# FFN input GEMMs by one level of Strassen for all 1024 tokens, the residual kept in DRAM tiles

## The chip, the cores and the metric

One NeuronCore of a Trainium2 chip runs the whole program. The metric is the device time of one execution in microseconds; a lower time is better.

## The reference

One encoder layer on x of 1024 tokens by 1024 features, all in float32. FFN1, a mixer, FFN2 and a last RMSNorm follow each other:

```python
def swiglu(x, w_in, w_out):
    gate, up = jnp.split(x @ w_in, 2, axis=-1)
    return (jax.nn.silu(gate) * up) @ w_out
...
x = x + 0.5 * swiglu(rmsnorm(x, ffn1_norm_g[l]), ffn1_w_in[l], ffn1_w_out[l])
...
x = x + merged @ w_mix_out[l]
x = x + 0.5 * swiglu(rmsnorm(x, ffn2_norm_g[l]), ffn2_w_in[l], ffn2_w_out[l])
...
return rmsnorm(x, final_norm_g)
```

`w_in` is 1024 by 5632 (gate columns, then up columns), `w_out` 2816 by 1024. The mixer (an mLSTM branch and a gating branch) lies between the two FFNs and is not touched.

## The kernel before, in words

Activations stand with features on the 128 partitions and 512 tokens along a row, so the sequence is done in two halves of 512 tokens. Each float32 operand is split into a high and a low float32r part (`split`, and `load_unit` for weights: one ScalarE cast and one VectorE subtraction), and a product is three matmuls (`PROD`: high by high, high by low, low by high). One matmul has a 128x128 piece of weights as the loaded operand and 128x512 activations as the streamed one.

`ffn` (L256) runs once for each half and each FFN, four times in all. It goes through 22 tiles of 128 hidden features in three blocks of 8, 8 and 6 (`BLOCKS`). `ffn_in` (L239) takes two tiles at once: 8 feature tiles of x by 3 matmuls, for two gate and two up banks of PSUM, then Silu on ScalarE (L244), the product on VectorE (L250) and a `split`. After a block the output projection accumulates in PSUM over the block's tiles (L271), and VectorE adds it to the residual `xs`, which stays in SBUF (L275). The last block of the last half goes in two parts of 256 tokens (`parts=2`), so that the end is short.

Work that isn't needed at once goes into the list `todo` and is taken from it by `spread`, one piece between two blocks of matmuls: the transposes of x, the normalisation of the next half (`normed`, `later=True`). RMS statistics are gathered by `Stats` (squares on ScalarE, sums on VectorE); `rstd` and `bcast` then make a chain of two small TensorE steps with small VectorE and ScalarE steps between (L198 to L221). All DMA is issued by SyncE (SP). A scheduler orders each engine's instructions by priority and by free buffers; each engine then runs its own list in that order and waits at an instruction whose operands or buffers are not ready.

Of the kernel before, what the change touches and what calls it, by code (L numbers as in the profile page):

```python
# [19 lines left out]
BLOCKS = [(0, 8), (8, 8), (16, 6)]  # L20
# [9 lines left out]
def block_body(ctx, tc, x, ffn1_norm_g, ffn1_w_in, ffn1_w_out, mix_norm_g, w_mix_in, mlstm_conv_w,  # L30
# [9 lines left out]
    wp = ctx.enter_context(tc.tile_pool(name="wp", bufs=3))  # L40
    bigp = ctx.enter_context(tc.tile_pool(name="bigp", bufs=16))
    tp = ctx.enter_context(tc.tile_pool(name="tp", bufs=5))
# [12 lines left out]
    open_psum(f1, 1, mm=3, po=3, ml=2)  # L55

    def t512():
        return tp.tile([P, NH], F32, tag="t512", name="t512")

    def psm():  # L60
        return bank("ml")

    def load_tokens(h):
        ts = []
        for t in range(4):
            xt = bigp.tile([P, D], F32, tag="big", name="xtok")
            nc.sync.dma_start(out=xt, in_=x[h * NH + t * P:h * NH + (t + 1) * P, :])
            ts.append(xt)
        return ts
# [31 lines left out]
    xd = [[tc.dram_tile([P, KT, NH], F32, name=f"xd{s}{h}") for h in range(2)] for s in range(2)]  # L101

    def load_unit(w_rows, ks, c0, extra=None):
# [9 lines left out]
        w = wp.tile([P, 2, n, nc_], F32R, tag="w", name="w")  # L113
# [4 lines left out]

    PROD = ((0, 0), (0, 1), (1, 0))
# [65 lines left out]
    class Stats:  # L185
# [25 lines left out]
        def bcast(self):  # L211
# [7 lines left out]
            bc = sp.tile([P, NH], F32, tag="bc", name="bc", bufs=1)  # L219
# [19 lines left out]
    def ffn_in(w_in, f0, xn, hp, ready=None):  # L239
        gb = feature_pair(w_in, f0 * P, xn, "mm", ready=ready)  # L240
        sg = []
        for j in range(2):
            t = t512()
            A.activation(out=t, in_=gb[j], func=AF.Silu)  # L244
            sg.append(t)
        ub = feature_pair(w_in, DFF + f0 * P, xn, "mm")
        hs = []
        for j in range(2):
            hf = t512()
            V.tensor_tensor(out=hf, in0=sg[j], in1=ub[j], op=ALU.mult)  # L250
            h = hp.tile([P, 2, NH], F32R, tag="h", name="h")
            split(hf, h)
            hs.append(h)
        return hs

    def ffn(w_in, w_out, xn, xs, hp, final, hooks={}, ready=None, parts=1):  # L256
        for bi, (f0, n) in enumerate(BLOCKS):
            hs = []
            for f in range(f0, f0 + n, 2):
                hs += ffn_in(w_in, f, xn, hp, ready if f == 0 else None)  # L260
                spread()
                spread()
            if bi in hooks:
                hooks[bi]()
            last = bi == len(BLOCKS) - 1
            np_ = parts if last else 1
            kg = tuple(tuple(range(a, min(a + 4, n))) for a in range(0, n, 4))
            for part in range(np_):
                ts = slice(part * NH // np_, (part + 1) * NH // np_)
                for d in range(0, KT, 2):  # L270
                    ob = feature_pair(w_out[f0 * P:(f0 + n) * P, :], d * P, hs, "po", kg, ts=ts)  # L271
                    spread()
                    for j in range(2):
                        xt = xs[d + j][:, ts]
                        V.scalar_tensor_tensor(out=xt, in0=ob[j], scalar=0.5, in1=xt, op0=ALU.mult, op1=ALU.add)  # L275
                        if last:
                            final(d + j, part, xt)
# [3 lines left out]

    wsT = cst.tile([P, 4, P], F32, name="wsT")
    t1 = cst.tile([P, KT, P], F32, name="t1")
    future = cst.tile([P, P], F32, name="future")
    bif = cst.tile([P, 8], F32, name="bif")
    nc.sync.dma_start(out=bif[:, 0:4], in_=mlstm_b_igate[0].partition_broadcast(P))
    nc.sync.dma_start(out=bif[:, 4:8], in_=mlstm_b_fgate[0].partition_broadcast(P))

    def setup():
        wraw = t512()  # L290
        nc.sync.dma_start(out=wraw.rearrange("p (g s) -> p g s", g=4), in_=sgu_w_s[0].rearrange("g t s -> t g s"))
        ps = psm()
        for g in range(4):
            PE.transpose(out=ps[:, g * P:(g + 1) * P], in_=wraw[:, g * P:(g + 1) * P], identity=ident)
        V.tensor_copy(out=wsT.rearrange("p g t -> p (g t)"), in_=ps)
        G.memset(wsT[64:P, :, 0:64], 0.0)
        bsb = t512()
        nc.sync.dma_start(out=bsb, in_=sgu_b_s[0].rearrange("g t -> (g t)").partition_broadcast(P))
        ps = psm()
        PE.matmul(out=ps, lhsT=ones, rhs=wsT.rearrange("p g t -> p (g t)"), start=True, stop=True)  # L300
        for ct in range(KT):
            g = ct // 2
            V.scalar_tensor_tensor(out=t1[:, ct, :], in0=ps[:, g * P:(g + 1) * P], scalar=pc("sb", ct),
                                   in1=bsb[:, g * P:(g + 1) * P], op0=ALU.mult, op1=ALU.add)
        G.memset(future, 0.0)
        G.affine_select(out=future, in_=future, compare_op=ALU.is_ge, fill=1e30, base=0, pattern=[[1, P]],
                        channel_multiplier=-1)

    def mix(mx, xnm):
# [305 lines left out]
        for half in range(2):  # L615
            xn = xnm[half]
            if half == 0:
                gz, gt = sgu_v(xn)
# [184 lines left out]
```

## Time and profile before

| | |
|---|---|
| runs | 2406.90, 2407.29, 2408.02 us, median 2407.29 |
| profiled execution, span | 2406.5 us |
| TensorE (PE) busy | 2383.2 us, 99% |
| weight loads (PEld) busy | 2012.1 us, 84% |
| VectorE (DVE) busy | 1174.0 us, 49% |
| ScalarE (ACT) busy | 890.1 us, 37% |
| GpSimd (POOL) busy | 3.9 us |
| DMA | 253.69 MB, 105 GB/s |

The span is the time from the first to the last instruction of the one execution that the profiler recorded; the median of the runs is 0.8 us above it. Busy time counts every instruction but register, branch, semaphore and DMA-issuing ones. Weight loads run under the matmuls.

### The profile page before, as it was taken

The numbers are of one execution on the slowest core, as the hardware profiler recorded it, in microseconds if no ns is written. First come the engines' busy times: TensorE is split into PE (matmuls) and PEld (weight loads), VectorE is DVE, ScalarE is ACT, GpSimd is POOL, SyncE is SP. The second block draws the span as 40 slices with busy tenths as digits, with TensorE's granted clock in tenths as the row PEclk, the third lists the DMA queues.
The fourth block names the chain that finished last, engine by engine and source line by source line (L and its number), as shares of the span: only waits on it lengthen the run. The fifth ranks groups of instructions, "written<-read, shape, count | busy, mean of one in ns | idle before, by whom it ended". The sixth has DMA issues, their size and how long they took to land. (4 is left out here: it accounts for less than half of the span.)

```text
span 2406.5 us, 28857 instructions
## 1 busy us (share of the span) xinstructions
PE 2383.2 (99%) x11817; PEld 2012.1 (84%) x11817; DVE 1174.0 (49%) x1864; ACT 890.1 (37%) x1178; POOL 3.9 (0%) x15
## 2 busy tenths in 40 slices
PE   8999999999999999999999999999999999999998
PEld 7888888888888988888889888888888888888887
DVE  4444434344335657556646666564344335333336
ACT  4223223323224445444434554453323223222224
POOL 0000000000000000000000000000000000000000
PEclk9999999999999999999999999999999999999999
DMA  5322324333324324332352342327333334333333
GB/s 176 92 92 91 98 87 136 105 97 97 96 88 141 97 79 123 97 87 81 95 160 80 96 123 80 101 75 227 97 96 97 97 92 127 106 97 98 97 93 123
DMA packets 240547, 253.69 MB, mean 105 GB/s; under 512 B 11160, under 2 KB 227864, under 8 KB 240416
## 3 DMA queue, kind: packets, MB, share of 16 engines
q1 hardware_dynamic: 240416, 251.86, 34.7%
q8 instruction: 92, 1.51, 0.3%
q14 instruction: 39, 0.32, 0.0%
HBM read 239.21 MB, written 12.62 MB: 105 GB/s over the span
## 5 line engine op out<-in xcount | busy, mean ns | idle before, releaser
L138 PE MATMUL mm<-xn,w 128*128 128x512 f32 x6528 | 1510.7, 390 | 0.5 <-DVE w L115 0.5
L138 PEld LDWEIGHTS mm<-xn,w 128*128 128x128 f32 x6528 | 1218.5, 188 | 249.5 <-issue 1.4
L115 DVE TENSOR_TENSOR w<-raw,w 128x1024 fp32r<-128x1024 f32 (+2 forms) x426 | 508.5, 1194 | 844.6 <-ACT w L114 844.3
L114 ACT CAST w<-raw 128x1024 fp32r<-128x1024 f32 (+2 forms) x426 | 436.9, 1026 | 882.4 <-PE mm L138 320.3
L138 PE MATMUL po<-h,w 128*128 128x512 f32 (+1 forms) x2256 | 493.0, 378 | 0.0
L138 PEld LDWEIGHTS po<-h,w 128*128 128x128 f32 x2256 | 403.6, 188 | 80.7 <-issue 0.5
L152 PE MATMUL mm<-w,xn 128*128 128x256 f32 x1344 | 164.8, 283 | 0.3
L152 PEld LDWEIGHTS mm<-w,xn 128*128 128x128 f32 x1344 | 162.9, 192 | 1.4 <-DVE w L115 0.7
L244 ACT ACTIVATE t<-mm 128x512 f32<-128x512 f32 x88 | 52.6, 598 | 152.5 <-PE mm L138 152.5
L275 DVE SCALAR_TENSOR_TENSOR x<-po,x 128x512 f32<-128x512 f32 (+1 forms) x104 | 66.8, 649 | 82.8 <-PE po L138 82.7
L171 ACT CAST h<-t 128x512 fp32r<-128x512 f32 x88 | 54.3, 618 | 106.2 <-DVE t L250 106.2
L138 PE MATMUL po<-mh,w 128*128 128x512 f32 x384 | 87.5, 389 | 0.0
L250 DVE TENSOR_TENSOR t<-t,mm 128x512 f32<-128x512 f32 x88 | 60.5, 687 | 50.0 <-PE mm L138 50.0
L138 PEld LDWEIGHTS po<-mh,w 128*128 128x128 f32 x384 | 71.9, 188 | 14.9
L172 DVE TENSOR_TENSOR h<-t,h 128x512 fp32r<-128x512 f32 x88 | 60.5, 687 | 30.4 <-ACT h L171 30.3
L453 DVE SCALAR_TENSOR_TENSOR t<-pre,par,t 128x512 f32<-128x512 f32 x96 | 72.0, 750 | 2.2
L575 ACT ACTIVATE t<-mm 128x512 f32<-128x512 f32 x48 | 28.7, 598 | 48.0 <-PE mm L138 47.9
L448 ACT COPY pre<-mm 128x512 f32<-128x512 f32 x32 | 18.8, 587 | 61.1 <-PE mm L138 61.1
L577 DVE TENSOR_TENSOR M<-M,t 128x512 f32<-128x512 f32 x32 | 22.1, 690 | 33.2 <-ACT t L575 33.2
L196 DVE TENSOR_TENSOR acc<-acc,t 128x512 f32<-128x512 f32 (+1 forms) x56 | 34.6, 618 | 4.4 <-ACT t L195 4.3
L575 ACT ACT_TABLE_LOAD x25 | 32.1, 1283 | 0.4
L171 ACT CAST xn<-t 128x512 fp32r<-128x512 f32 x40 | 24.3, 619 | 21.1 <-DVE t L229 20.9
(180 smaller groups left out, 1048.5 us busy)
## 6 DMA issues: line engine op xcount, KB each, us to landing
raw<-in_ffn_w_in_dram SPq DMA_DIRECT2D x176, 512.0 KB, 3.5
raw<-in_w_mix_in_dram SPq DMA_DIRECT2D x124, 512.0 KB, 3.8
raw<-in_ffn_w_out_dram SPq DMA_DIRECT2D x84, 512.0 KB, 3.4
xr<-xd SPq DMA_DIRECT2D x32, 256.0 KB, 3.6
raw<-in_w_mix_out_dram SPq DMA_DIRECT2D x16, 512.0 KB, 4.3
raw<-in_ffn_w_out_dram SPq DMA_DIRECT2D x20, 256.0 KB, 3.1
xtok<-in_x_dram SPq DMA_DIRECT2D x8, 512.0 KB, 5.9
xd<-x SPq DMA_DIRECT2D x16, 256.0 KB, 3.1
```

Of the source, the lines that this page charges most:

```text
L114: A.copy(out=w[:, 0, 0:n, :], in_=raw[:, 0:n, :])
L115: V.tensor_tensor(out=w[:, 1, 0:n, :], in0=raw[:, 0:n, :], in1=w[:, 0, 0:n, :].bitcast(F32), op=ALU.subtract)
L138: PE.matmul(out=banks[j], lhsT=w[:, a, i, j * P:(j + 1) * P], rhs=act[k][:, b, ts], start=(k == first and pi == 0), stop=(k == last and pi ...
L152: PE.matmul(out=o, lhsT=act[k][:, b, t * P:(t + 1) * P], rhs=w[:, a, i, :], start=(t % 2 == 0 and k == 0 and pi == 0), stop=(t % 2 == 1 an ...
L171: A.copy(out=dst[:, 0, :], in_=src)
L172: V.tensor_tensor(out=dst[:, 1, :], in0=src, in1=dst[:, 0, :].bitcast(F32), op=ALU.subtract)
L196: V.tensor_tensor(out=self.acc, in0=self.acc, in1=sq, op=ALU.add)
L244: A.activation(out=t, in_=gb[j], func=AF.Silu)
L250: V.tensor_tensor(out=hf, in0=sg[j], in1=ub[j], op=ALU.mult)
L275: V.scalar_tensor_tensor(out=xt, in0=ob[j], scalar=0.5, in1=xt, op0=ALU.mult, op1=ALU.add)
L453: V.scalar_tensor_tensor(out=t, in0=pre[:, j:j + NH], scalar=pc("cw%d" % j, cc), in1=t, op0=ALU.mult, op1=ALU.add)
L575: A.activation(out=t, in_=b[j], func=fn)
```

## The change

Both halves of the sequence now go through an FFN together, in the new class `Ffn`. For a tile f of 128 hidden features the input GEMM is a 2x2 block product: the rows are gate and up, the inner blocks are the two halves of the 1024 features, the columns are the two halves of the tokens. Strassen's scheme in Winograd's form takes seven block products of 12 matmuls in place of eight. `operands` builds sums and differences of the activation blocks (`t1` to `t4`) once per FFN; `group` builds those of the weight blocks (`s1` to `s4`) for each tile and adds the products up on VectorE. For the first five tiles `first_product` computes two of the seven products ahead, while the operands are being built. The hidden tiles go in blocks of 3 (and 2), and `down` adds a block's output projection to a residual that lies in DRAM tiles: for each of 16 tiles of 128x512, GpSimd issues a load (L366) into a buffer of the pool `cp` and a store (L369) out of it. The last block (`last`) keeps the tiles in SBUF. The bits of the diff that carry this:

```diff
-BLOCKS = [(0, 8), (8, 8), (16, 6)]
+NF = DFF // P
+BLOCKS = [(0, 3), (3, 3), (6, 3), (9, 3), (12, 3), (15, 3), (18, 2), (20, 2)]
+AHEAD = 5
...
+        xv = x[h * NH:(h + 1) * NH, :].rearrange("(t p) d -> p t d", p=P)
+        for i in range(4):
+            xt = bigp.tile([P, 4, 2, P], F32, tag="big", name="xtok")
+            for j in range(2):
+                nc.sync.dma_start(out=xt[:, :, j, :], in_=xv[:, :, (4 * j + i) * P:(4 * j + i + 1) * P])
...
-    xd = [[tc.dram_tile([P, KT, NH], F32, name=f"xd{s}{h}") for h in range(2)] for s in range(2)]
+    xd = [[[tc.dram_tile([P, NH], F32, name=f"xd{s}{h}{d}") for d in range(KT)] for h in range(2)] for s in range(3)]
...
+            self.tx, self.hp, self.wp, self.sp_ = pool("tx", 12), pool("hp", 8), pool("fw", 4), pool("fs", 3)
+            self.cp = pool("cp", 6)
...
+        def raw(self, f, d, both):
+            r = rawp.tile([P, 4, 2, P], F32, tag="raw", name="raw")
+            rs = slice(d * NH, (d + 1) * NH)
+            for j in range(2 if both else 1):
+                nc.sync.dma_start(out=r[:, :, j, :], in_=self.w_in[rs, j * DFF + f * P:j * DFF + (f + 1) * P]
+                                  .rearrange("(k p) c -> p k c", p=P))
+            return r
+
+        def unit(self, src, n=4):
+            w = self.wp.tile([P, 2, n, P], F32R, tag="fw", name="fw")
+            A.copy(out=w[:, 0], in_=src)
+            V.tensor_tensor(out=w[:, 1], in0=src, in1=w[:, 0].bitcast(F32), op=ALU.subtract)
+            return w
+
+        def prod(self, bank, w, b, start, stop):
+            for i in range(4):
+                for pi, (x, y) in enumerate(PROD):
+                    PE.matmul(out=bank, lhsT=w[:, x, i, :], rhs=self.B[b][i][:, y, :],
+                              start=(start and i == 0 and pi == 0), stop=(stop and i == 3 and pi == 2),
+                              skip_group_check=True)
+
+        def combine(self, a, b, op):
+            s = self.sp_.tile([P, 4, P], F32, tag="s", name="s")
+            V.tensor_tensor(out=s, in0=a, in1=b, op=op)
+            return s
+
+        def first_product(self, f):
+            e = self.hp.tile([P, 2, NH], F32, tag="h", name="early")
+            r1, r2 = self.raw(f, 0, False), self.raw(f, 1, False)
+            w1, w2 = self.unit(r1[:, :, 0, :]), self.unit(r2[:, :, 0, :])
+            a = bank("mm")
+            self.prod(a, w1, "11", True, False)
+            A.copy(out=e[:, 0, :], in_=a)
+            self.prod(a, w2, "21", False, True)
+            A.activation(out=e[:, 1, :], in_=a, func=AF.Silu)
+            self.early[f] = e
+
+        def group(self, f):
+            r1, r2 = self.raw(f, 0, True), self.raw(f, 1, True)
+            a11, a21 = evens(r1)
+            a12, a22 = evens(r2)
+            e = self.early.pop(f, None)
+            if e is None:
+                w = self.unit(a11)
+                a = bank("mm")
+                self.prod(a, w, "11", True, False)
+                p1 = self.c512()
+                A.copy(out=p1, in_=a)
+            else:
+                p1 = e[:, 0, :]
+            s1 = self.combine(a21, a22, ALU.add)
+            s2 = self.combine(s1, a11, ALU.subtract)
+            w = self.unit(s2)
+            b = bank("mm")
+            self.prod(b, w, "t2", True, True)
+            u2 = self.c512()
+            V.tensor_tensor(out=u2, in0=b, in1=p1, op=ALU.add)
+            if e is None:
+                w = self.unit(a12)
+                self.prod(a, w, "21", False, True)
+                sg1 = self.c512()
+                A.activation(out=sg1, in_=a, func=AF.Silu)
+            else:
+                sg1 = e[:, 1, :]
+            yield
+            s3 = self.combine(a11, a21, ALU.subtract)
+            w = self.unit(s3)
+            b = bank("mm")
+            self.prod(b, w, "t3", True, True)
+            u3 = self.c512()
+            V.tensor_tensor(out=u3, in0=b, in1=u2, op=ALU.add)
+            w = self.unit(s1)
+            d = bank("mm")
+            self.prod(d, w, "t1", True, False)
+            c22 = self.c512()
+            V.tensor_tensor(out=c22, in0=d, in1=u3, op=ALU.add)
+            w = self.unit(a22)
+            b = bank("mm")
+            self.prod(b, w, "t4", True, True)
+            V.tensor_tensor(out=u3, in0=b, in1=u3, op=ALU.add)
+            h1 = self.hp.tile([P, 2, NH], F32R, tag="h", name="h")
+            V.tensor_tensor(out=u3, in0=u3, in1=sg1, op=ALU.mult)
+            split(u3, h1)
+            s4 = self.combine(a12, s2, ALU.subtract)
+            w = self.unit(s4)
+            self.prod(d, w, "22", False, True)
+            V.tensor_tensor(out=u2, in0=d, in1=u2, op=ALU.add)
+            A.activation(out=u2, in_=u2, func=AF.Silu)
+            h2 = self.hp.tile([P, 2, NH], F32R, tag="h", name="h")
+            V.tensor_tensor(out=c22, in0=c22, in1=u2, op=ALU.mult)
+            split(c22, h2)
+            self.hs.append((h1, h2))
+            yield
+
+        def down(self, f0, n, hs, src, dst):
+            for d in range(0, KT, 2):
+                raw = rawp.tile([P, n, 2 * P], F32, tag="raw", name="raw")
+                nc.sync.dma_start(out=raw, in_=self.w_out[f0 * P:(f0 + n) * P, d * P:(d + 2) * P]
+                                  .rearrange("(k p) c -> p k c", p=P))
+                for j in range(2):
+                    w = self.unit(raw[:, :, j * P:(j + 1) * P], n)
+                    for t in range(2):
+                        xt = self.c512()
+                        G.dma_start(out=xt, in_=src[t][d + j])
+                        o = self.down_mm(w, n, [h[t] for h in hs], slice(0, NH))
+                        V.scalar_tensor_tensor(out=xt, in0=o, scalar=0.5, in1=xt, op0=ALU.mult, op1=ALU.add)
+                        G.dma_start(out=dst[t][d + j], in_=xt)
...
+
+        def down_mm(self, w, n, hs, ts):
+            o = bank("mm")[:, ts]
+            for i in range(n):
+                for pi, (x, y) in enumerate(PROD):
+                    PE.matmul(out=o, lhsT=w[:, x, i, :], rhs=hs[i][:, y, ts], start=(i == 0 and pi == 0),
+                              stop=(i == n - 1 and pi == 2))
+            return o
+
+        def last(self, f0, n, hs, src, final, parts, hook):
...
+            for t in range(2):
+                xl = []
+                for part in range(parts[t]):
+                    ts = slice(part * NH // parts[t], (part + 1) * NH // parts[t])
+                    for d in range(KT):
+                        if part == 0:
+                            if d % 2 == 0:
+                                xl.append(self.tx.tile([P, 2, NH], F32, tag="tx", name="xl"))
+                            G.dma_start(out=xl[-1][:, d % 2, :], in_=src[t][d])
+                        o = self.down_mm(ws[d], n, [h[t] for h in hs], ts)
+                        xt = xl[d // 2][:, d % 2, ts]
+                        V.scalar_tensor_tensor(out=xt, in0=o, scalar=0.5, in1=xt, op0=ALU.mult, op1=ALU.add)
+                        final(t, d, part, xt)
+                        spread()
+                hook(t, [xl[d // 2][:, d % 2, :] for d in range(KT)])
+
+        def run(self, src, final, parts, hook):
+            self.hs = []
+            blocks = list(BLOCKS)
+            pend = None
+            for bi, (f0, n) in enumerate(blocks):
+                for f in range(f0, f0 + n):
+                    g = self.group(f)
+                    next(g)
+                    if pend is not None:
+                        self.down(*pend)
+                        pend = None
+                    next(g)
...
+                hs, self.hs = self.hs, []
+                if bi < len(blocks) - 1:
+                    pend = (f0, n, hs, src if bi == 0 else xd[2], xd[2])
+                else:
+                    self.last(f0, n, hs, xd[2], final, parts, hook)
+
+        def operands(self, i, get):
+
+            b12, b22, b11, b21 = get(0, i, 1), get(1, i, 1), get(0, i, 0), get(1, i, 0)
+
+            def put(key, src):
+                pool, tag = (self.tx, "tx") if key in ("t1", "t2", "t3") else (bigp, "big")
+                t = pool.tile([P, 2, NH], F32R, tag=tag, name="b")
+                split(src, t)
+                self.B.setdefault(key, []).append(t)
+
+            t3 = self.c512()
+            V.tensor_tensor(out=t3, in0=b22, in1=b12, op=ALU.subtract)
+            put("t3", t3)
+            V.tensor_tensor(out=b12, in0=b12, in1=b11, op=ALU.subtract)
+            put("t1", b12)
+            V.tensor_tensor(out=t3, in0=b22, in1=b12, op=ALU.subtract)
+            put("t2", t3)
+            V.tensor_tensor(out=b21, in0=b21, in1=t3, op=ALU.subtract)
+            put("22", b22)
+            put("t4", b21)
...
+        tok[1] = load_tokens(1)
+        ffn1.first_product(0)
+        scales(1)
+        for i in range(4):
+            ffn1.first_product(i + 1)
+            for d in (i, i + 4):
+                residual(0, d)
+                residual(1, d)
+            ffn1.operands(i, get)
...
+        def get2(j, i, t):
+            b = ffn2.c512()
+            d = 4 * j + i
+            G.dma_start(out=b, in_=xd[1][t][d])
+            V.scalar_tensor_tensor(out=b, in0=b, scalar=pc("g2", d), in1=bcs[t], op0=ALU.mult, op1=ALU.mult)
+            return b
+
+        ffn2.first_product(0)
+        for i in range(4):
+            ffn2.first_product(i + 1)
+            ffn2.operands(i, get2)
```

Three places show how the order of instructions moves. In its rows the part ahead of the arrow is written, the part behind it read; a number behind a name tells one buffer from another.

TensorE where FFN1 ends and the mixer begins, of the kernel before: `h` is the hidden tile, `xn` the normalised input of the mixer, `acc` the statistics of the second half.

```order
L138 MATMUL mm<-xn,w 128x512 x384
L138 MATMUL po<-h,w 128x512 x192
L138 MATMUL mm<-xn,w 128x512 x288
L138 MATMUL po<-h,w 128x512 x144
L165 MATMUL mm<-w,xn 128x264 x22
L201 MATMUL ml<-ones,acc 128x1 x4
L165 MATMUL mm<-w,xn 128x264 x30
L218 MATMUL ml<-t_4980,ones 128x512
```

The same place of the changed kernel:

```order
L280 MATMUL mm<-b,fw 128x512 x48
L376 MATMUL mm<-h,wl 128x512 x66
L210 MATMUL ml<-ones,acc 128x1 x4
L376 MATMUL mm<-h,wl 128x512 x25
L227 MATMUL ml<-t_5856,ones 128x512
L376 MATMUL mm<-h,wl 128x512 x5
L174 MATMUL mm<-w,xn 128x264 x8
L210 MATMUL ml<-ones,acc 128x1 x4
L174 MATMUL mm<-w,xn 128x264 x17
```

The statistics of the first half now come inside the last 96 matmuls of FFN1 and not half an FFN earlier, and the first mixer GEMM follows 5 matmuls behind the broadcast of its scale.

TensorE where the mixer ends and FFN2 begins, of the kernel before (`mh` is the mixer's output):

```order
L138 MATMUL po<-mh,w 128x512 x192
L138 MATMUL mm<-xn,w 128x512 x14
L201 MATMUL ml<-ones,acc 128x1 x4
L138 MATMUL mm<-xn,w 128x512 x17
L218 MATMUL ml<-t_12813,ones 128x512
L138 MATMUL mm<-xn,w 128x512 x353
```

The same place of the changed kernel; `fw` are weight units, `b` the operands that `operands` builds:

```order
L147 MATMUL po<-mh,w 128x512 x192
L210 MATMUL ml<-ones,acc 128x1 x4
L227 MATMUL ml<-t_13900,ones 128x512
L280 MATMUL mm<-xn,fw 128x512 x120
L280 MATMUL mm<-b,fw 128x512 x192
L376 MATMUL mm<-h,fw 128x512 x144
```

No FFN matmul stands any more between the mixer's last matmul and the two small steps of the statistics; 120 matmuls stand between these and the first one that needs the built operands.

GpSimd's queue in the second `down` of FFN1 (before, GpSimd issued no DMA); `xd_148` and its like are residual tiles in DRAM, `c` a buffer of `cp`:

```order
L366 DMA c<-xd_148 128x512
L366 DMA c<-xd_156 128x512
L366 DMA c<-xd_149 128x512
L366 DMA c<-xd_157 128x512
L369 DMA xd_148<-c 128x512
L369 DMA xd_156<-c 128x512
L366 DMA c<-xd_150 128x512
L369 DMA xd_149<-c 128x512
L366 DMA c<-xd_158 128x512
L369 DMA xd_157<-c 128x512
```

Four loads go ahead; from there a load stands behind the store of the tile three before its own, and its buffer is free when the store of the tile four before has landed.

## Rows read from the trace of the kernel before

**Rows 1.** Page: engines' busy us (share) xinstructions; clock granted in 40 slices.

```profile
PE 2383.2 (99%) x11817; PEld 2012.1 (84%) x11817; DVE 1174.0 (49%) x1864; ACT 890.1 (37%) x1178; POOL 3.9 (0%) x15
...
PEclk9999999999999999999999999999999999999999
```

**Rows 2.** Longest wait of TensorE in the program: us, times, longest.

```profile
PE po L675 <- DVE dg L671: 8.1, 1, 8.1
```

**Rows 3.** Busy us by engine in three stretches; then clock, DMA share, GB/s.

```profile
0.00:20.00 20.00, 10.89 (x68) 10.22 (x69) 8.77 (x38) 11.57 (x29) 1.31 (x10) 1.00 0.54 187
100.00:700.00 600.00, 599.96 (x2662) 494.19 (x2661) 247.83 (x307) 177.70 (x221) 0.40 (x2) 1.00 0.32 99
2360.00:2406.50 46.50, 37.82 (x312) 36.15 (x310) 32.66 (x81) 20.95 (x40) 0.00 (x0) 0.95 0.44 136
```

**Rows 4.** TensorE's groups by form: busy us, mean ns, idle before.

```profile
L138 PE MATMUL mm<-xn,w 128*128 128x512 f32 x6528 | 1510.7, 390 | 0.5 <-DVE w L115 0.5
...
L138 PE MATMUL po<-h,w 128*128 128x512 f32 x1968 | 455.7, 392 | 0.0
...
L138 PE MATMUL po<-h,w 128*128 128x256 f32 x288 | 37.3, 283 | 0.0
...
L752 PE MATMUL ml<-ident,x 128*128 128x128 f32 x64 | 11.3, 282 | 0.7 <-DVE x L275 0.6
...
L218 PE MATMUL ml<-t,ones 128*128 128x512 f32 x10 | 5.2, 600 | 0.3 <-DVE gT L413 0.3
...
L675 PE MATMUL ml<-dg,xtok 128*128 128x128 f32 x32 | 4.2, 278 | 0.5 <-DVE xn L679 0.5
```

**Rows 5.** VectorE's groups by form: busy us, mean ns, idle before.

```profile
L275 DVE SCALAR_TENSOR_TENSOR x<-po,x 128x512 f32<-128x512 f32 x88 | 60.6, 691 | 80.4 <-PE po L138 80.3
...
L250 DVE TENSOR_TENSOR t<-t,mm 128x512 f32<-128x512 f32 x88 | 60.5, 687 | 50.0 <-PE mm L138 50.0
...
L196 DVE TENSOR_TENSOR acc<-acc,t 128x512 f32<-128x512 f32 x42 | 28.8, 685 | 4.3 <-ACT t L195 4.2
...
L229 DVE SCALAR_TENSOR_TENSOR t<-x,par,bc 128x512 f32<-128x512 f32 x24 | 17.1, 744 | 2.3 <-ACT bc L220 2.3
...
L115 DVE TENSOR_TENSOR w<-raw,w 128x512 fp32r<-128x512 f32 x20 | 13.8, 692 | 46.2 <-ACT w L114 46.2
...
L275 DVE SCALAR_TENSOR_TENSOR x<-po,x 128x256 f32<-128x256 f32 x16 | 6.2, 418 | 2.4 <-PE po L138 2.4
```

**Rows 6.** ScalarE's groups by form: busy us, mean ns, idle before.

```profile
L114 ACT CAST w<-raw 128x512 fp32r<-128x512 f32 x20 | 12.4, 621 | 63.6 <-issue 42.6 <-PE mm L138 15.6 <-PE po L138 5.4
```

**Rows 7.** DMA issues of 256 KB to or from the residual, us to landing.

```profile
xr<-xd SPq DMA_DIRECT2D x32, 256.0 KB, 3.6
...
xd<-x SPq DMA_DIRECT2D x16, 256.0 KB, 3.1
...
xd<-xr SPq DMA_DIRECT2D x16, 256.0 KB, 5.3
x<-xd SPq DMA_DIRECT2D x16, 256.0 KB, 4.7
```

**Rows 8.** Timeline of the start: start us, us, engine, line, [idle].

```profile
11.81 0.29 DVE L671 TENSOR_SCALAR dg<-ident,r 128x128 f32<-128x128 f32 x1
...
19.76 21.61 PE L138 MATMUL mm<-xn,w 128*128 128x512 f32 x94 [0.53 <-DVE w L115]
```

**Rows 9.** Timeline, end of the mixer: last statistics add to broadcast.

```profile
1665.41 0.68 DVE L196 TENSOR_TENSOR acc<-acc,t 128x512 f32<-128x512 f32 x1
...
1668.75 0.88 DVE L215 TENSOR_SCALAR t<-ident,rstd 128x128 f32<-128x128 f32 x4
...
1672.16 0.59 ACT L220 COPY bc<-ml 128x512 f32<-128x512 f32 x1 [1.35 <-PE ml L218]
```

**Rows 10.** Timeline, start of the mixer: VectorE beside a GpSimd memset.

```profile
758.02 2.39 DVE L215 TENSOR_SCALAR t<-ident,rstd 128x128 f32<-128x128 f32 x4
...
758.34 1.93 POOL L323 MEMSET v<- 128x2064 f32 x1 [275.29 <-DMA xd<-x]
```

More of the change, by code (lines that the diff above doesn't have):

```diff
@@ L237, in normed @@
         return res
[L239 to L260, printed above, removed]
-                spread()
[L262 to L271, printed above, removed]
-                    spread()
[L273 to L277, printed above, removed]
+    def evens(src):
+        return src[:, :, 0, :], src[:, :, 1, :]
@@ L279, in block_body @@
     wmi = w_mix_in[0]
     CQ, CK_, CV, CO, CI, CU, CZV, CGM, CGS = 0, 1024, 2048, 3072, 4096, 4104, 5128, 6152, 7176
[L282 to L307, printed above, removed]
@@ L706, in block_body, with scaled @@
-        xnm = [None, None]
-        bcs = [None, None]
-        def third():
-            setup()
-            xnm[0] = normed(xs[0], "gm", bcs[0], True)
-        ready = first()
-        ffn(ffn1_w_in[0], ffn1_w_out[0], xns[0], xs[0], hp, fin1(0), {0: second}, ready)
-        bcs[0] = st2[0].bcast()
-        ffn(ffn1_w_in[0], ffn1_w_out[0], xns[1], xs[1], hp, fin1(1), {0: third})
-        xnm[1] = st2[1].bcast()
+            dgs.append(dg)
+        def scaled(h, d):
+            ps = psm()
+            for t in range(4):
+                PE.matmul(out=ps[:, t * P:(t + 1) * P], lhsT=tok[h][d % 4][:, t, d // 4, :],
+                          rhs=dgs[h][:, t * P:(t + 1) * P], start=(t == 0), stop=(t == 3), skip_group_check=True)
+            return ps
@@ new lines, in residual, with get @@
+        def residual(h, d):
+            ps = psm()
+            for t in range(4):
+                PE.transpose(out=ps[:, t * P:(t + 1) * P], in_=tok[h][d % 4][:, t, d // 4, :], identity=ident)
+            xt = t512()
+            V.tensor_copy(out=xt, in_=ps)
+            G.dma_start(out=xd[1][h][d], in_=xt)
+        def get(j, i, t):
+            b = ffn1.c512()
+            A.activation(out=b, in_=scaled(t, 4 * j + i), func=AF.Copy, scale=pc("g1", 4 * j + i))
+            return b
+        scales(0)
@@ new lines, in block_body @@
+        for d in range(KT):
+            ps = scaled(0, d)
+            xt = bigp.tile([P, 2, NH], F32R, tag="big", name="xn")
+            A.activation(out=xt[:, 0, :], in_=ps, func=AF.Copy, scale=pc("g1", d))
+            V.scalar_tensor_tensor(out=xt[:, 1, :], in0=ps, scalar=pc("g1", d), in1=xt[:, 0, :].bitcast(F32),
+                                   op0=ALU.mult, op1=ALU.subtract)
+            xns.append(xt)
+        ffn1.B["11"], ffn1.B["21"] = xns[:4], xns[4:]
+        tok[1] = load_tokens(1)
```

229 lines of the change are left out of this document (121 added, 108 removed).

## The prediction

> **What bounds the kernel now.** I read the page's busy times first: TensorE is busy for 2383.2 of 2406.5 us and the clock is at its upper level, 2.4 GHz, in all 40 slices [rows 1]. The list of its waits shows one that counts, 8.1 us at the start [rows 2]. By stretches the idle time lies in the first 20 us (9.1 us) and the last 46.5 (8.7 us), where the mean granted clock is 0.95; in 600 us of FFN1 it is 0.04 us, with VectorE at 41%, ScalarE at 30% and DMA at 32% of its time [rows 3]. So TensorE's stream of instructions is the time, and two things move it: the matmuls taken out, and the holes made in a stream that has none.
>
> **TensorE's work.** A 128x512 matmul takes 1510.7 / 6528 = 0.2314 us [rows 4]. The input GEMMs have 22 x 96 x 2 = 4224 of them now; with 22 x 84 x 2 = 3696, 528 go: -122.2 us. The output projection keeps its products, but the piece in 256-token parts shrinks from 288 matmuls to 96: +96 x 0.2316 - 192 x 0.1295 = -2.6 us [rows 4]. The second half of x is now scaled by float32 matmuls as the first was (`scaled`): 64 more, each two records in the trace of 4.2 / 32 = 0.131 us [rows 4], +16.8 us. One broadcast goes, two records, -1.0 us [rows 4]. Sum: -109.0 us of work.
>
> **The steady group.** Per feature tile TensorE has 84 matmuls, 19.4 us; VectorE has 7 weight subtractions, 4 sums and 9 steps on products, 20 at about 0.69 us [rows 5] = 13.8 us; ScalarE less than that. In the order a weight unit is made three products (8.3 us) before it is used. I count no hole. The first five groups lack two products: 13.9 us of TensorE against 18 x 0.69 = 12.4 us of VectorE, tight, still none. DMA carries some 4.3 MB per 30.5 us (with the projection), 142 GB/s; from 0.32 at 99 GB/s [rows 3] that is near half its time.
>
> **The residual through DRAM.** Of the 14 calls of `down`, 12 have 9 matmuls per tile, 2.08 us, and 2 have 6, 1.39 us; 16 tiles each. A buffer is loaded, added to (0.69 us [rows 5]), stored, and loaded again, and four are in turn: one tile per (load + store + 0.69) / 4. The trace has no GpSimd DMA. For 256 KB through SP it has loads of 3.6 and 4.7 us and stores of 3.1 and 5.3 [rows 7]: 1.85 to 2.67 us per tile. Over the 12 tiles behind the four prefetched ones, the add falls behind by 12 x (period - 2.08), at most 7.1 us; with six PSUM banks TensorE can run some five tiles ahead, 10.4 us, so nothing is lost. With 1.39 us per tile it falls behind by 5.5 to 15.4 us against 7: I take 3.5 us for each of the two (period 2.27, the middle), so **+7** (0 to 18).
>
> The Trainium skill (DMA: Bandwidth & Descriptors, Anatomy of one DMA) fits a GpSimd DMA as 2.0 us plus bytes / 436e3, which would be 2.6 us for each of these, a period of 1.47, and nothing lost in any call; no row here shows it.
>
> **The start of FFN1.** Each token tile now holds a quarter of the features of all tokens, so no statistic is complete before all 2 MB have landed; then 12 of the 16 squares and the scale chain follow. Now the last scale is ready at 11.8 us and the matmuls run without a break from 19.8 [rows 8]. I take +9 us (5 to 13). Then five pairs of early products, the scaling, the transposes and the first `t2` product give TensorE about 54 us; up to that product's last operand VectorE has some 78 instructions: 73 at 0.69 and the small ones of the scales, 54 us, and ScalarE 60 at 0.62 [rows 6], 37, with 16 half-width squares and five table loads, as much again as VectorE. Both feed each other, so I take 62 us, 8 of them holes. **+17** (6 to 28).
>
> **From FFN1 to the mixer.** Before, the mixer's input for the first half was made under the second half of FFN1. Now, after the last scale, VectorE has 8 normalisations (0.744), 8 subtractions, 7 sums for the statistics and 3 adds left: 18.4 us [rows 5], while TensorE has 5 matmuls of FFN1 and 3 us of mixer products that it can do as inputs come. **+16** (10 to 22).
>
> **From the mixer to FFN2.** The statistics' two steps now follow the mixer's last matmul with nothing between, where 31 matmuls stood. From the last add to the broadcast took 7.3 us [rows 9]; with the square before it and three VectorE steps now queued inside, about 10. Only then can VectorE build operands: 14 scalings at 0.744, 36 sums and subtractions, 9 weight units and 3 sums at 0.69: 43.5 us. Against it stand 120 early matmuls, 27.8 us, and most of the first `t2` product, 2. Holes: 10 + 43.5 - 30 = 23.5, and some for loads that wait for one of six `c` buffers: **+25** (15 to 32).
>
> **The end.** Before, 18 half-width matmuls (2.3 us) per tile hid the steps on it. Now it is 6, 0.78 us, and two transposes of 0.177 [rows 4], against three VectorE steps of 0.42 [rows 5], 1.26 us: over the 16 half tiles 2.1 us, and over the first half's 8 tiles about nothing; the 12 output scalings, the statistics chain and the loads behind freed buffers add the rest. **+10** (5 to 15).
>
> **Sum.** -109 + 7 + 17 + 16 + 25 + 10 = -34 us. The profiled span is 0.8 us below the median; against the median: **2373 us**. The low ends give -73 (2334), the high ends +6 (2413).
>
> **The rivals.**
> *The holes are hidden* (0.17). If engines overlap better than my sums of one engine, and the first `t2` matmuls run as operands come, 22 us of holes stay and it is 2407 - 109 + 22 = 2320. For it: TensorE waited 0.04 us in 600, behind chains as long. Against: the order puts nothing else between.
>
> *The queue of GpSimd decides* (0.17, the other side). All 448 loads and stores of `down` go through one queue, in order, and a store that waits for its add holds up the loads behind it. From a period of 3.05 us (load plus store 11.5 us, or 1.52 us of issue for each) it is no gain: 12 x 0.97 - 10.4 = 1.24 us in each of 12 calls and 12 x 1.66 - 7 = 12.9 in each of two make 41 us in place of 7, which is the 34. At 3.3 it is 12 x 4.24 + 2 x 15.9 = 83, so 2373 + 76 = 2449. For it: the trace's slower stores and loads already make 2.67, and GpSimd has done nothing like it. Where it worked, the engines got in each other's way: four scalings of VectorE that take 0.88 us [rows 9] took 2.39 beside a 1.93 us memset [rows 10]. Against: VectorE's work in FFNs is nearly all of the two-operand kind, not of this one.
>
> The Trainium skill has the rule that would make this so (SBUF — State Buffer, SBUF: two separate sides): a GpSimd DMA's descriptors wait while VectorE runs in a two-port mode. By that rule FFN stages of two-operand steps leave the queue alone; the memset row agrees that the two engines block each other.
>
> **How the numbers follow.** The forecast has 0.66, each rival 0.17. The forecast's own range is 2334 to 2413. Within 0.2% (about what a measurement of this kernel can tell from no change, 4.8 us) is the forecast's upper end, 0.06; the first rival and the rest of the forecast make it faster, 0.77; the second rival makes it slower, 0.17. The range for 8 in 10 runs from the first rival to short of the second's price, 2322 to 2440. If a hole also drops the clock to its lower level, as the 0.95 of the last slice hints, a few us come on top; that lies within it.
>
> **What would show it.** Right: 3696 matmuls on the lines of `prod` at 0.231 us, TensorE's busy time near 2274 us, and holes in four places, each behind VectorE: before the first `t2` products of FFN1 and FFN2, before the mixer's first GEMM, and in the last 50 us. Within blocks it is busy throughout, and the adds of `down` (L368) wait for a load at most for a few us. Wrong: TensorE waiting inside each block behind L368, with loads and stores of GpSimd that take over 5.8 us each; holes at the weight units, from 512-byte rows that land late; or a matmul rate that is not 0.231 us because of more traffic in SBUF.

## The result, and the profile after

The changed kernel takes 2439.5 us (median of 4, 2428.5 to 2440.5) against 2407.7: a ratio of 1.0122 (95% interval 1.0101 to 1.0143). It is slower by 32 us; the forecast was 34 faster, 2373 us. The page of the changed kernel, its first two parts:

```profile
span 2437.0 us, 30372 instructions
## 1 busy us (share of the span) xinstructions
PE 2334.6 (96%) x11311; PEld 1934.9 (79%) x11311; DVE 1494.3 (61%) x2655; ACT 907.9 (37%) x1458; POOL 287.6 (12%) x543
...
PEclk9999999999998999999999999999899999999998
```

The span less TensorE's busy time is 102.4 us of holes; the kernel before had 23.3 [rows 1], and the forecast added 75, so the holes came to what was forecast in all. The busy time did not: 2274 was forecast, 2334.6 is there. The same execution by stretches (PE busy first; behind POOL the mean granted clock, DMA share and GB/s):

```profile
0.00:96.00 96.00, 75.35 (x420) 61.68 (x420) 60.17 (x152) 62.93 (x148) 9.64 (x24) 1.00 0.48 143
96.00:724.00 628.00, 614.33 (x2645) 499.16 (x2646) 374.61 (x595) 171.43 (x302) 124.74 (x232) 0.99 0.48 149
724.00:800.00 76.00, 60.58 (x354) 52.55 (x352) 57.04 (x134) 34.13 (x53) 15.69 (x31) 0.87 0.47 156
800.00:1680.00 880.00, 877.93 (x4814) 748.40 (x4813) 536.93 (x987) 418.48 (x563) 0.56 (x1) 1.00 0.34 99
1680.00:1760.00 80.00, 61.09 (x235) 46.16 (x234) 58.50 (x100) 33.06 (x57) 7.99 (x15) 0.85 0.45 132
1760.00:2380.00 620.00, 602.80 (x2593) 490.61 (x2592) 363.81 (x575) 167.62 (x295) 120.51 (x224) 0.99 0.48 147
2380.00:2437.00 57.00, 42.51 (x261) 36.37 (x259) 43.29 (x117) 20.25 (x44) 8.49 (x16) 0.89 0.44 148
```

Holes stand in the steady blocks of both FFNs too, 13.7 and 17.2 us, and there, at the transitions and at the end the mean granted clock is below 1; in the first 96 us, with 20.7 us of holes, it is 1.00. The list of TensorE's waits names them:

```profile
PE mm L280 <- DVE c L338: 23.1, 11, 4.8
PE ml L102 <- DMA t<-in_mlstm_conv_w_dram: 14.1, 1, 14.1
PE mm L174 <- DVE xl L403: 12.4, 1, 12.4
PE ml L227 <- DVE t L224: 10.1, 2, 8.1
PE mm L280 <- ACT fw L273: 7.7, 2, 7.0
PE mm L376 <- DVE c L368: 7.7, 3, 3.9
```

The groups of TensorE that answer to [rows 4] (busy time behind the bar):

```profile
L280 PE MATMUL mm<-b,fw 128*128 128x512 f32 x2640 | 636.9, 398 | 32.4 <-DVE c L338 23.1 <-ACT fw L273 7.7 <-ACT b L180 1.0
L147 PE MATMUL mm<-xn,w 128*128 128x512 f32 x2304 | 558.4, 396 | 0.0
L376 PE MATMUL mm<-h,fw 128*128 128x512 f32 x1920 | 442.6, 392 | 7.7 <-DVE c L368 7.7
L280 PE MATMUL mm<-xn,fw 128*128 128x512 f32 x1056 | 266.6, 400 | 1.9 <-ACT early L295 1.9
L147 PE MATMUL po<-mh,w 128*128 128x512 f32 x384 | 90.0, 395 | 0.0
```

The last row is the clue. `po<-mh` is the mixer's output GEMM, which the diff does not touch and which has no hole and full clock: 384 matmuls took 87.5 us before and take 90.0 now. The rows of the kernel before, the second of its mixer alone (760 to 1660 us):

```profile
L138 PE MATMUL po<-mh,w 128*128 128x512 f32 x384 | 87.5, 389 | 0.0
...
L138 PE MATMUL mm<-xn,w 128*128 128x512 f32 x2304 | 545.6, 391 | 0.0
```

`mm<-xn,w` takes 558.4 / 2304 = 0.2424 us for each, and took 0.2368; the matmuls over h, beside the heaviest traffic, 442.6 / 1920 = 0.2305. The starts of single matmuls of 512 columns in the trace, those less than 260 ns apart, follow each other by 226.9 ns over h and by 233.3 over xn and mh.

What differs is where the operands lie. The program's table of addresses (bytes within a partition) has xn before the change at 61632 and `w` at 37056, each 192 modulo 256 bytes. The change drops a pool and moves constants, so that xn lies at 30368 (160 modulo 256), the mixer's `w` at 203648 (128) and the FFNs' `fw` at 192992 (224). Only h and the splits t1, t2, t3 are at 224 as `fw` is, and only they are fast.

So there were two suspects: the place of the operands, and the residual's tiles behind the waits on L338 and L368.

### The profile page after: what moved, and what is told of

It reads as the page before. It is cut to its first block, busy times and chain, and to the rows that moved or that the text cites. A ratio compares the mean times of both kernels' runs of the same rounds, so it can differ in the third digit from the quotient of the medians.

```text
span 2437.0 us, 30372 instructions
## 1 busy us (share of the span) xinstructions
PE 2334.6 (96%) x11311; PEld 1934.9 (79%) x11311; DVE 1494.3 (61%) x2655; ACT 907.9 (37%) x1458; POOL 287.6 (12%) x543
## 5 line engine op out<-in xcount | busy, mean ns | idle before, releaser
L280 PE MATMUL mm<-b,fw 128*128 128x512 f32 x2640 | 636.9, 398 | 32.4 <-DVE c L338 23.1
L280 PEld LDWEIGHTS mm<-b,fw 128*128 128x128 f32 x2640 | 500.7, 190 | 153.9 <-issue 20.2
L147 PE MATMUL mm<-xn,w 128*128 128x512 f32 x2304 | 558.4, 396 | 0.0
L147 PEld LDWEIGHTS mm<-xn,w 128*128 128x128 f32 x2304 | 425.9, 188 | 96.1
L376 PE MATMUL mm<-h,fw 128*128 128x512 f32 x1920 | 442.6, 392 | 7.7 <-DVE c L368 7.7
L376 PEld LDWEIGHTS mm<-h,fw 128*128 128x128 f32 x1920 | 362.8, 189 | 84.9 <-issue 8.0
L368 DVE SCALAR_TENSOR_TENSOR c<-mm,c 128x512 f32<-128x512 f32 x224 | 154.4, 691 | 266.1 <-DMA c<-xd 161.1
L123 DVE TENSOR_TENSOR w<-raw,w 128x1024 fp32r<-128x1024 f32 (+2 forms) x146 | 176.5, 1209 | 150.1 <-ACT w L122 149.9
L280 PE MATMUL mm<-xn,fw 128*128 128x512 f32 x1056 | 266.6, 400 | 1.9 <-ACT early L295 1.9
L280 PEld LDWEIGHTS mm<-xn,fw 128*128 128x128 f32 x1056 | 199.0, 190 | 52.6 <-ACT early L295 4.1
L366 POOL DMA_DIRECT2D c<-xd x224 | 121.1, 541 | 839.5 <-DVE h L181 533.2
L122 ACT CAST w<-raw 128x1024 fp32r<-128x1024 f32 (+2 forms) x146 | 151.2, 1037 | 157.1 <-PE mm L147 89.0
L274 DVE TENSOR_TENSOR fw<-raw,fw 128x512 fp32r<-128x512 f32 (+2 forms) x244 | 149.9, 616 | 48.5 <-ACT fw L273 48.2
L161 PE MATMUL mm<-w,xn 128*128 128x256 f32 x1344 | 162.7, 282 | 0.2
L161 PEld LDWEIGHTS mm<-w,xn 128*128 128x128 f32 x1344 | 160.8, 188 | 1.5 <-DVE w L123 0.6
L274 DVE TENSOR_TENSOR fw<-s,fw 128x512 fp32r<-128x512 f32 x176 | 120.7, 686 | 56.6 <-ACT fw L273 56.1
L369 POOL DMA_DIRECT2D xd<-c x224 | 121.0, 540 | 163.2 <-DVE c L368 156.2
```

The costliest lines, as they stand in the source:

```text
L122: A.copy(out=w[:, 0, 0:n, :], in_=raw[:, 0:n, :])
L123: V.tensor_tensor(out=w[:, 1, 0:n, :], in0=raw[:, 0:n, :], in1=w[:, 0, 0:n, :].bitcast(F32), op=ALU.subtract)
L147: PE.matmul(out=banks[j], lhsT=w[:, a, i, j * P:(j + 1) * P], rhs=act[k][:, b, ts], start=(k == first and pi == 0), stop=(k == last and pi ...
L161: PE.matmul(out=o, lhsT=act[k][:, b, t * P:(t + 1) * P], rhs=w[:, a, i, :], start=(t % 2 == 0 and k == 0 and pi == 0), stop=(t % 2 == 1 an ...
L274: V.tensor_tensor(out=w[:, 1], in0=src, in1=w[:, 0].bitcast(F32), op=ALU.subtract)
L280: PE.matmul(out=bank, lhsT=w[:, x, i, :], rhs=self.B[b][i][:, y, :], start=(start and i == 0 and pi == 0), stop=(stop and i == 3 and pi == 2),
```

## The experiments

### The place of the operands

**FFN phase.** A pool changes its place in the order:

```diff
     rawp = ctx.enter_context(tc.tile_pool(name="rawp", bufs=3))
+    sp = ctx.enter_context(tc.tile_pool(name="sp", bufs=2))
     bigp = ctx.enter_context(tc.tile_pool(name="bigp", bufs=16))
...
-    sp = ctx.enter_context(tc.tile_pool(name="sp", bufs=2))
```

> The changed kernel with the pool of small tiles opened ahead of the pool of xn instead of behind it; nothing else. The start of xn (and of b12's and b22's splits) modulo 128 bytes goes from 32 to 96, which is that of the weights fw in both FFNs; the mixer's w stays at 0. In the trace of the changed kernel the matmuls over xn and those two splits start 233.4 ns apart, those over the other three splits and over h, which stand at 96 as fw does, 226.9. Phase theory (a matmul streams faster where its two operands start at the same place modulo 128 bytes): the 2112 matmuls over this pool in the FFNs go from 233.4 to 227 ns, 13.7 us less, 2426; the mixer's 2304 over xn stay at 233 or near it. Address theory (the place of the moving operand alone decides, 32 bad, 64 and 96 good): the mixer's go to 227 as well, 31 us less, 2408. Contention theory (the added transfers and VectorE work slow the streams): no change, 2439.

Measured: 2421.0 us (2420.0 to 2423.8). The matmuls over xn in the FFNs follow each other by 227.2 ns, those of the mixer by 233.4 still. That xn is at 96 modulo 128 now and the mixer's GEMMs stay slow speaks against the address theory, and that a move changes the speed at all against contention. Some 5 us of the 18.5 are not the matmuls' own: the mean granted clock rose from 0.982 to 0.986.

**All phase.** The edit above, and 96 bytes ahead of the mixer's weights:

```diff
         ss = pool("ss", 1)
+        pool("pd", 1).tile([P, 24], F32, tag="pd", name="pd")
         wpool[0] = pool("wp", 3)
```

> The kernel of the FFN-phase run with 96 unused bytes ahead of the mixer's weight pool, so that w starts at 96 modulo 128 as xn and mh now do. Phase theory: the mixer's 2304 + 384 matmuls of 512 columns go from 233.3 to 227 ns, 17 us less than the FFN-phase run, 2408 to 2410, and the mixer takes the 910 us that it took before the change. Address theory: the same as the FFN-phase run, since xn doesn't move. Contention theory: 2439.

Measured: 2408.6 us (2401.4 to 2413.3), ratio to before 1.0005 (0.9995 to 1.0015). The mixer's rows are back where they were before the change, 545.2 / 2304 = 0.2366 us for each:

```profile
L147 PE MATMUL mm<-xn,w 128*128 128x512 f32 x2304 | 545.2, 390 | 0.0
L147 PE MATMUL po<-mh,w 128*128 128x512 f32 x384 | 87.5, 389 | 0.0
...
L161 PE MATMUL mm<-w,xn 128*128 128x256 f32 x1344 | 164.8, 283 | 0.2
```

The two rows of 512 columns gave 15.9 us, and 12.4 came of it. Against them stand the waits on L338, which grew from 26.6 to 30.8 us, and the matmuls of 256 columns on L161, which stream `w` against xn and went from 162.5 to 164.8. Both edits together give back 31 us, with not one instruction changed.

**Before, apart.** The kernel before, with 32 bytes between `w` and xn:

```diff
     wp = ctx.enter_context(tc.tile_pool(name="wp", bufs=3))
+    ctx.enter_context(tc.tile_pool(name="pd", bufs=1)).tile([P, 8], F32, tag="pd", name="pd")
     bigp = ctx.enter_context(tc.tile_pool(name="bigp", bufs=16))
```

> The kernel before the change with 32 unused bytes between the pool of weights and the pool of xn: xn and mh go from 64 to 96 modulo 128, h from 0 to 32, w stays at 64. Nothing else changes. Phase theory: 6912 matmuls over xn and mh go from 227 to 233.3 ns and 1968 over h from 229 to 233.3, 52 us more, 2459. Address theory: xn stays fast at 96, h at 32 goes to 233.3, 8 us more, 2416. Contention theory: no change, 2407.

Measured: 2455.5 us, ratio 1.0202 (1.0187 to 1.0217). 32 unused bytes cost 48 us, more than the whole change. The rows (one line number further down) against those of the kernel before: +40.1, +8.4 and +2.5 us.

```profile
L139 PE MATMUL mm<-xn,w 128*128 128x512 f32 x6528 | 1550.8, 396 | 0.5 <-DVE w L116 0.5
L139 PE MATMUL po<-h,w 128*128 128x512 f32 x1968 | 464.1, 396 | 0.0
...
L139 PE MATMUL po<-mh,w 128*128 128x512 f32 x384 | 90.0, 395 | 0.0
```

**Before, 64 bytes.** Which distance counts? h in the kernel before was slightly slow, 229.0 ns:

```diff
-    sp = ctx.enter_context(tc.tile_pool(name="sp", bufs=2))
+    sp = ctx.enter_context(tc.tile_pool(name="sp", bufs=2)); sp.tile([P, 16], F32, tag="pd", name="pd", bufs=1)
```

> The kernel before the change with 64 unused bytes between the pools of xn and h, so that h starts at 64 modulo 128 as w does; xn is there already. Phase theory: the 1968 matmuls over h go from 229.0 to 226.9 ns, 4 us less, 2403. Any other theory: no change, 2407.

Measured: 2414.8 us, ratio 1.0035 (1.0021 to 1.0048): slower, a miss. The matmuls over h went to 233.2 ns, 463.7 us in place of 455.7 [rows 4], all of the difference:

```profile
L138 PE MATMUL po<-h,w 128*128 128x512 f32 x1968 | 463.7, 396 | 0.0
```

Agreement modulo 128 is not the rule.

**Before, 192 bytes.** The same edit with 48 numbers in place of 16.

> The kernel before the change with 192 unused bytes between the pools of xn and h, so that h starts at 1216 modulo 2048 and w at 192 (before the change 1024 and 192, in the 64-byte run 1088 and 192). Modulo 128 the 64-byte run agreed and was slow, so agreement modulo 128 is not enough. All the fast pairs so far agree modulo 512 as well. Phase theory so mended: the matmuls over h go from 229.6 to 227 ns, 5 us less than before, 2402. If only the place of h itself counts, or another thing that the unused bytes move (the mixer's tiles shift by as much): 2407 or more.

Measured: 2402.5 us, ratio 0.9981 (0.9972 to 0.9990). The rule so mended holds:

```profile
L138 PE MATMUL po<-h,w 128*128 128x512 f32 x1968 | 451.3, 390 | 0.0
...
L138 PE MATMUL po<-h,w 128*128 128x256 f32 x288 | 38.1, 287 | 0.0
```

**Four, 256 bytes.** The last-four kernel (below) with 88 numbers in place of 24 ahead of the mixer's weights.

> The last-four kernel with 352 instead of 96 unused bytes ahead of the mixer's weights: w goes from 992 to 1248 modulo 2048 against 480 of xn and mh, so that they agree modulo 256 and no longer modulo 512. If 512 bytes are what counts, the mixer's 2304 + 384 matmuls go from 227 to 233 ns, 17 us more, 2358; if 256, 2341 as before.

Measured: 2341.8 us against 2341.3, and 545.2 us on the mixer's row. So 256 bytes count. All pairs of the study with 512 columns, by the start of the moving (streamed) operand less that of the stationary (loaded) one:

| difference modulo 256 | where | start to start, ns |
|---|---|---|
| 0 | before: xn, mh; after: h with `fw`, t1 to t3; all that was mended | 226.7 to 227.7 |
| 0 | the last block's h with `wl`, after and mended | 227.7 to 228.4 |
| 64 | before: h | 229.0 |
| 32 | after: xn and mh of the mixer; before, apart: xn, mh | 233.2 to 233.3 |
| 96 | FFN phase: xn, mh of the mixer; before, apart: h | 233.3 to 233.4 |
| 128 | before, 64 bytes: h | 233.2 |
| 192 | after: xn and the splits of b22 and t4 in the FFNs (the first expectation says b12 and b22) | 233.3 to 233.4 |

Matmuls of 256 columns do not follow it. L161 takes 164.8 us where the two operands agree and 162.7 and 162.5 where they are 32 and 96 bytes apart. The 288 over h take 38.1 us at a difference of 0, 37.3 at 64 [rows 4], 38.2 at 96 and 37.9 at 128. What in the engine makes the rule is not shown.

### The tiles of the residual

The timeline of the changed kernel at the end of one output pass (start, duration, engine):

```profile
435.82 5.68 PE L280 MATMUL mm<-b,fw 128*128 128x512 f32 x24
436.04 0.54 POOL L366 DMA_DIRECT2D c<-xd  x1 [1.77 <-DMA xd<-c]
...
440.49 0.69 DVE L368 SCALAR_TENSOR_TENSOR c<-mm,c 128x512 f32<-128x512 f32 x1 [2.36 <-DMA c<-xd]
...
442.43 0.68 DVE L333 TENSOR_TENSOR c<-mm,c 128x512 f32<-128x512 f32 x1
...
443.63 0.68 DVE L338 TENSOR_TENSOR c<-mm,c 128x512 f32<-128x512 f32 x1
...
444.46 4.58 PE L280 MATMUL mm<-b,fw 128*128 128x512 f32 x12 [2.95 <-DVE c L338]
```

To be read from below: TensorE has run out of the products t3, t1 and t4 and may add the next one to c22's bank only when VectorE has read it (L338). That read stands in VectorE's queue behind the last add of the residual (L368), which waits for a load (L366), which was issued only when the store of the tile's last user had landed. The three products take 8.4 us (the second row is of another pass):

```profile
433.10 8.40 PE L280 MATMUL mm<-b,fw 128*128 128x512 f32 x36
...
258.48 3.04 PE L280 MATMUL mm<-b,fw 128*128 128x512 f32 x12 [1.07 <-DVE c L338]
```

The last add starts 7.4 us after they do, L338 ends 3.8 us after that, so some 2.8 us are lost. The hole of 2.95 us is paid for a second time, in part: the 12 matmuls behind it take 4.58 us, where they take 3.04 behind the hole of 1.07 at the other pass. From 444 to 449 us the mean granted clock is 0.66.

**Slots.** Two tiles that live across the pass leave the shared pool of six; line numbers stay as they are:

```diff
-                p1 = self.c512()
+                kept = self.hp.tile([P, 2, NH], F32, tag="h", name="kept") if hold else None; p1 = kept[:, 0, :] if hold else self.c512()
...
-            u2 = self.c512()
+            u2 = p1 if hold else self.c512()
...
-                sg1 = self.c512()
+                sg1 = kept[:, 1, :] if hold else self.c512()
```

(`hold` is true for the first group of a block that has a pass to run.)

> The changed kernel with u2 and silu(g1) of the group that waits over the output pass kept in an h tile instead of in two tiles of the pool of six that the residual's loads share, so that six instead of four are left to the residual. Same work, same addresses of the operands. Slots theory: a residual tile is held for its load, 3.7 us, the update, 0.7, and the store, 3.8, and waits besides, some 9.5 us; with four the pass does one output per 2.4 us where TensorE needs 2.05, with six 1.6. The waits of TensorE behind the update c22, 23.1 us, and behind the residual's update, 7.7, go to under 10 together, and with them most of the 60 matmuls at half clock behind them (0.2 us each): 20 to 33 us less, 2406 to 2419. Rival (VectorE has too much to do around the output pass, and the loads only seem to hold it): the waits stay, 2435 to 2442.

Measured: 2402.0 us (2398.9 to 2408.2), ratio 0.9981 (0.9971 to 0.9990): 37 us less, beyond the range. Adds follow each other for the most part by 2.04 us, in place of about 2.7 in the starved part of a pass. VectorE's wait for loads in the changed kernel:

```profile
DVE c L368 <- DMA c<-xd: 161.1, 106, 3.8
```

and with six tiles for the residual, with TensorE's wait on L338:

```profile
DVE c L368 <- DMA c<-xd: 37.5, 22, 3.0
...
PE mm L280 <- DVE c L338: 6.0, 2, 3.3
```

TensorE's waits on L338 fell from 23.1 to 6.0 and those on L368 from 7.7 to 1.2: 24 us. The other 13 are for the most part the clock: 0.986 of 2402.5 us in place of 0.982 of 2437.0, 67 us at the lower level in place of 88.

**Five tiles.** `self.cp = pool("cp", 6)` becomes 5.

> The changed kernel with five tiles instead of six in the pool that the residual's loads share, so that three are left to them; no other address moves. Slots theory: one output per 9.5 / 3 = 3.2 us where TensorE needs 2.05; over the 12 outputs behind the first ones each pass falls behind by some 10 us more than with four tiles, and TensorE's waits behind the residual's update and c22 rise from 31 us to over 100: over 2500. Rival (VectorE's work decides, not the tiles): within 10 us of 2439.

Measured (one run): 2496.5 us, slower by 57 as the tiles would have it and not as the rival would. It is a little under the forecast, and TensorE's waits are well under it, 57.6 + 11.2 us in place of over 100:

```profile
PE mm L280 <- DVE c L338: 57.6, 14, 6.0
...
PE mm L376 <- DVE c L368: 11.2, 5, 5.0
```

The rest is for the most part the clock, whose mean fell from 0.982 to 0.973. Three, four and six tiles give 2496, 2439 and 2402.

### Both, and the transitions

**Both.** The edits of all phase and of slots.

> The two edits together: the addresses of the all-phase run and the six residual tiles of the slots run. The two causes are separate if their gains add: 31 us (phase) and 37 us (slots) off 2439 make 2371 (2366 to 2376), which is the forecast of the sum before the two costs. If the waits behind the residual are partly what the slower streams made of them, or the other way round, the sum is less: 2385 or more.

Measured: 2371.9 us (2370.7 to 2373.4), ratio 0.9857 (0.9844 to 0.9871). The two costs add up, 31 and 37 of 68 us.

**Last four.** Both, with

```diff
-BLOCKS = [(0, 3), (3, 3), (6, 3), (9, 3), (12, 3), (15, 3), (18, 2), (20, 2)]
+BLOCKS = [(0, 3), (3, 3), (6, 3), (9, 3), (12, 3), (15, 3), (18, 4)]
```

> The kernel of the both run with a last block of four feature tiles in place of two blocks of two. It removes one output pass of six-matmul outputs per FFN and gives each output of the last block 12 matmuls instead of 6, so that 8 outputs of a token half take 21.8 us instead of 10.9. Theory of the holes at the transitions (VectorE's statistics, normalisation and last updates have too little TensorE work beside them): the 12.6 us wait ahead of the mixer's first GEMM shrinks by up to 10.9, the half clock behind it by some 6 us of loss, the waits of the short passes (6 us) go, the end gains some 3; the half-width matmuls add 2.6: 2347 to 2360. Rival (the wait ahead of the mixer is the chain of the statistics behind the last output, whatever stands ahead of it): 2366 to 2373.

Measured: 2341.3 us (2338.7 to 2342.2), ratio 0.9728 (0.9715 to 0.9741), below the range that was expected. Against the run before, TensorE's holes went from 76.4 to 54.8 us and the mean granted clock from 0.987 to 0.994. The wait of 12.4 us ahead of the mixer is gone; its GEMM follows FFN1's last matmul:

```profile
714.62 5.15 PE L376 MATMUL mm<-h,wl 128*128 128x512 f32 x22
719.60 2.11 PE L174 MATMUL mm<-w,xn 128*128 128x264 f32 x16
722.66 1.02 PE L210 MATMUL ml<-ones,acc 128*128 128x1 f32 x8 [0.95 <-DVE acc L205]
```

**Late scale.** The last-four kernel, with the broadcast's matmuls moved behind early products:

```diff
-            return st.bcast()
+            return st
...
-                bcs.append(mix_out(0, prev))
+                bcs.append(mix_out(0, prev).bcast())
...
-        ffn2.first_product(0)
+        ffn2.first_product(0); bcs[1] = bcs[1].bcast()
```

> The last-four kernel with the broadcast of the second half's scale, ahead of FFN2, called behind the first early product instead of ahead of it: the matmuls of its statistics and of its broadcast stand 12 and 34 early matmuls later in TensorE's order. At this place TensorE waits for the statistics 2.7 us, for the broadcast 7.9 and, 120 early matmuls (27.2 us) later, for the operands of the first t2 product 7.6, and runs some 20 us at half clock. Theory that VectorE's queue is the bound here (scale, then four operand groups, 38 us): the early matmuls start 10 us sooner and the wait ahead of t2 grows by as much, 2338 to 2344. Theory that the order on TensorE is the bound: the 10.6 us go and with them the half clock behind them, 2326 to 2331.

Measured: 2340.0 us (2338.0 to 2341.6): no gain that can be told. The wait for the broadcast fell from 7.9 to 2.4 us, and a new one of 7.7 stands among the early products, on VectorE's weight splits (L274). The time is that of the theory of VectorE's queue. The wait came back earlier than this theory has it, though: the one ahead of the first t2 product did not grow, it fell from 7.6 to 5.7 us.

## Why the prediction was wrong, step by step

**TensorE's work** failed first, on its duration. TensorE was busy for 60 us more than forecast, 2334.6 in place of 2274. By the trace's records of the granted clock 27 of them were lost at 1.2 GHz (54 us of busy time at half speed). Of the other 33, the two placement edits took back 25 (the all-phase run is busy for 2299.7 us, 17 of them lost at 1.2 GHz); some 8 stay unexplained. The count was right: 3696 matmuls on L280. But they were costed at the kernel before's 0.2314 us, together with GEMMs that the diff does not touch, as if a matmul's time were its own property. It depends on how its two operands lie to each other, and the change moved both. That cost 31 us by the runs, with what the placement did to waits and clock. (0.2314 is besides a mean of 0.2368 in the mixer and 0.2285 in the FFNs, where the matmuls were taken out; that is worth 1.5 us.) The prediction named the sign of being wrong ("a matmul rate that is not 0.231 us because of more traffic in SBUF"), but the cause is not traffic: no transfer differs between 2439 and 2408.

**The residual through DRAM** failed on its price, +7 for what was worth 37. Load and store took 3.7 and 3.8 us, within [rows 7]. Two steps were wrong. The period was taken as 2.27 us from (load + store + add) / 4; it was about 2.7 once the prefetched tiles were used up. With the measured load, store and add the same formula gives 2.05, so the rest is time in which a tile waits for its turn, and the formula had none. And the cover was taken from the six PSUM banks, 10.4 us, which would have hidden 12 x (2.7 - 2.08) = 7.4 us even so. What TensorE needed was not a bank but L338, queued on VectorE behind the late adds, after 36 matmuls, 8.4 us, of which VectorE's own steps up to L338 take 3.8. So the longer passes lost time too: 10 of the 11 waits on L338 stand behind them. "Wrong: TensorE waiting inside each block behind L368" describes it, one step further down the queue.

The estimate from the Trainium skill (DMA: Bandwidth & Descriptors, Anatomy of one DMA) of 2.6 us for such a transfer disagrees with the 3.7 and 3.8 measured (medians; the fastest took 2.8 and 2.3). By it the prediction's sum would have lost nothing here.

**The other holes** were right in kind and place and somewhat dear. The growth of TensorE's idle time over the same stretches of the kernel before (9.1 us in the first 96, 0.04 and 0.03 in the blocks, 1.3, 0.2 and 8.7 in the others): start of FFN1 11.5 (forecast 17; 7.2 of it in the first 22 us, forecast 9), into the mixer 14.1 (16), into FFN2 18.7 (25), the end 5.8 (10). The blocks' 30.8 in place of 7 made up for it, which is why the sum of the holes looks right.

**The clock** was left as "a few us". The mean granted clock, 0.982 over 2437.0 us, makes (1 - 0.982) x 2 x 2437 = 88 us at 1.2 GHz, since a stretch at half clock lowers the mean by half its share. Of the 11 waits on L338 the five of 2.2 to 4.8 us were each followed by 3 to 7 us at the lower level, the six of 0.9 to 1.8 us were not; around the transitions it lasted 10 to 17.

**The rivals.** "The queue of GpSimd decides" came out nearest in time (2449) and is not shown as such: the period stayed under its 3.05 us, an issue takes 0.54 us, two per tile are 1.08 of the 2.05 that TensorE needs, and with the same queue and two tiles more the waits went. Its chain, in which a store that waits for its add holds up the loads behind it, may have a part in it with four tiles; no run shows that alone. GpSimd's stores wait for adds 156.2 us in the changed kernel and 166.2 with six tiles, where TensorE's waits on L338 and L368 are down to 7.2. "The holes are hidden" is excluded by the rows of the stretches.

With both costs mended the kernel takes 2371.9 against 2373 forecast, in part by luck: in its trace TensorE is busy for 2292.3 us, 18 more than forecast, most of it the lower clock, and the holes come to 53 in place of 75. Against the kernel before with its own 5 us of placement mended (2402.5), the whole change is then worth 31 us, and 61 with the last block of four.

## What to carry to other kernels

Before a trace's durations are carried over to a kernel whose pools change, look whether the operands' addresses change, and time rows that the diff does not touch first. In a stream without holes, follow each new wait to what is queued behind it on its engine, and count the tiles that a load and a store must share; add to a hole what the lower clock behind it costs, here 1.4 to 1.5 us in the 12 matmuls behind holes of 2.2 to 3.0 us.

## What was not expected of the hardware

A float32r matmul of 512 columns starts 226.9 ns after the last one where the moving and the stationary operand start at the same place modulo 256 bytes, 233.3 at differences of 32, 96, 128 and 192, and 229.0 at 64: 2.8% of the GEMMs' time, 48 us of this kernel for 32 unused bytes. In the same traces matmuls of 256 columns have no such gain. Why 64 bytes cost less than the others stays open, and so does whether other types behave so; no run tried that.
